# A hybrid S5 / neighbourhood-attention step on one core: a new order for its first stage

## The chip, the cores and the metric

The kernel runs on one core of one Trainium2 chip. The metric is the device time of one execution in microseconds (us). Five engines matter: PE (TensorE, matrix products, with PEld for its weight loads), DVE (VectorE), ACT (ScalarE), POOL (GpSimd) and SP (SyncE, which here only starts transfers). Each engine works through its own list of instructions in order; an instruction that waits for another engine or for a transfer holds up all that stands behind it in its list.

## The reference

One layer of a diffusion backbone for 384 tokens (256 of a sample, 128 of a prompt). What the change touches is the front of it: the modulation of the input by a condition, the root-mean-square norm, the first columns of the input projection, and the discretisation of the state-space tables.

```python
def _rms(x, w):
    y = xf * lax.rsqrt(jnp.mean(xf * xf, axis=-1, keepdims=True) + EPS)
    return (y * w.astype(jnp.float32)).astype(x.dtype)

def _modulation(cond, w_ada, b_ada):
    mod = jax.nn.silu(cond) @ w_ada + b_ada
    shift, scale, gate = jnp.split(mod[:, None, :], 3, axis=-1)

def _front(x, shift, scale, norm_w, w_in, q_norm_w, k_norm_w):
    h = _rms(x, norm_w) * (1 + scale) + shift
    proj = h @ w_in            # cut into u, z_s, q, k, v, z_a, g_s, g_a
    ...

def _s5_discretize(a_re, a_im, log_dt, b_re, b_im):
    lam = lax.complex(jnp.minimum(a_re.astype(f32), -1e-4), a_im.astype(f32))
    dt = jnp.exp(log_dt.astype(f32))[..., None]
    lam_bar = jnp.exp(lam * dt)
    b_bar = ((lam_bar - 1) / lam)[..., None] * b
    ...
```

Behind it come the state-space scan over u, the attention over q, k, v, gates from z_s, z_a, g_s and g_a, and the output projections. D_MODEL is 2048, the projection is 2048 x 10240, w_ada is 2048 x 6144, all in float32.

## The kernel before

**Precision.** Every float32 product of a weight w and an input h is made as three products of parts: `hi` (w rounded, by ACT) and `lo` (what is left, by a subtraction), and `hh`, `hl` of the input in the same way. So a step of the projection is hh·hi + hl·hi + hh·lo, lines 813, 814 and 815, each with a moving side of 384 tokens.

**First stage.** It makes u, z_s and half of g_s (3072 columns of `w_in`) while the modulation is still being computed. The contraction of 2048 is cut into nine slices: two of 128 rows (slices 0 and 1), then seven of 256 (slices 2 to 8). A slice's work is a list of units of 512 KB of `w_in` (2 units in slice 0, 4 in slice 1, 6 in each later one), each unit two half-units, each half-unit 12 products on PE. After them the result in PSUM (tile `m`, three buffers) goes to `ua`, `zs` or `gs`: copied in slices 0 and 1 where it is the first, added by DVE afterwards (line 147, `ua<-m,ua`). A slice's `hh` and `hl` need the modulation of that slice: products of the condition `ct` with `w_ada` (`ada_mm`, line 693, two or four groups a slice, one loaded tile `wa` each), a copy (`ada_sum`), a transpose (`ada_turn`, line 707), three small DVE operations (`ada_fin`), the modulation on ACT (`modulate`, tile `hf`), and the split into `hh` and `hl` (`split_h`, lines 731 and 147, both on DVE). The table `AHEAD` says in which half-unit n of a slice each of these steps for the next slice stands; `fn == "mm"` and `"turn"` come after the half-unit's products, the others before.

**Weights.** `Stream` loads `w_in` units into `raw` (four buffers), and `prep` makes `hi` on ACT and `lo` for each half-unit three half-units ahead; in this stage `lo` is made on POOL (`low_on_pool`), 128x512 each. All loads stand on SP's list: at the start x (tile `X`, three of 1 MB), five small vectors into `vn`, then `wa` and `raw` tiles. POOL's list begins with eleven small loads (the norm weights, and `a2`, `ld` for the tables). A transfer from SP, or ACT, takes one of eight semaphores in turn and waits until the earlier transfer on it has landed.

**Start.** ACT squares and sums each third of X (line 756), POOL takes the root, DVE scales X, PE turns all 16 column tiles of X (`turn_x`, line 775), copied back by ACT and DVE in turn. In this list stand the first two `ada_mm`, and behind all 16 tiles the first product of slice 0.

**Tables.** `ssm_setup` is a generator of some hundred DVE operations on 128x64 tiles (`expo`, sine and cosine, `cmul`). `Background` runs it: after every half-unit from slice 2 on `bg.step(0.6)` lets the generator go to its next `yield`, so that two to eight operations follow each other on DVE.

**End of the stage.** In slice 8 the finished `zs` and `gs` are gated: ACT takes the tanh of `zs` into a tile `sg` (a ring of six, shared), DVE makes the product into it, SP stores it (`zss`), two half-units after one another; `gs` likewise without the DVE step (`gss`). In the same half-units the state-space stage starts: `ssm_read` puts its loads on SP (C, then B in rows of 64 bytes into `x4b`, then U), between the `raw` units of the next block.

Behind the first stage come blocks of the projection and the output products, with the state-space scan and the attention beside them; the change leaves them as they are.

## Time and profile before

| what | value |
|---|---|
| time, median of 3 runs | 1227.48 us (1226.68 to 1229.29) |
| profiled execution, its own time | 1229.62 us |
| its span | 1227.8 us |
| PE busy | 1165.2 us (95%), 7215 products |
| DVE / ACT / POOL busy | 817.4 / 565.7 / 158.6 us |
| first product of slice 0 | 31.48 us into the span |
| end of the first stage | about 300 us |
| transfers | 217.38 MB, mean 177 GB/s |

The page lists each engine's busy time, the chain of work that ended last, the costliest groups of instructions and the transfers; the views behind it show single instructions in order of time with the idle time before each and what ended it. The profiled time lies 2.1 us above the median of the runs; differences are made against the profiled execution.

### The profile page before, as it was taken

The page shows a single profiled execution, that of the slowest core. Times are in us where ns is not written, and L with a number is a line of the kernel's source. Part 1 is how long each engine was busy: PE and PEld are TensorE (multiplying, and loading weights), DVE is VectorE, ACT ScalarE, POOL GpSimd, SP SyncE. Part 2 cuts the span into 40 slices and gives each one's busy share as a digit, 9 for nine tenths or more (in the row PEclk, how much of TensorE's full clock was granted, in tenths as well). Part 3 has the DMA queues.
Part 4 walks back from the last instruction along what each step waited for, and adds up shares of the span by engine and source line. Part 5 has one row for each costly group of instructions (what it writes and reads, how often), then busy time and mean ns, then how long its engine had stood idle before and what let it go on. Part 6 is the DMA issues. An engine that isn't in the chain of part 4 may idle for free.

```text
span 1227.8 us, 19705 instructions
## 1 busy us (share of the span) xinstructions
PE 1165.2 (95%) x7215; PEld 1016.4 (83%) x7215; DVE 817.4 (67%) x1957; ACT 565.7 (46%) x1027; POOL 158.6 (13%) x126
## 2 busy tenths in 40 slices
PE   3999999998999999999999999999898999999997
PEld 2787788897889888889999778877697899878886
DVE  3588775555649993454999344468778855687873
ACT  4432223334683339677334944455545433343332
POOL 2444444453000000000000001100100000000000
PEclk9999999998999999999999999999999999999999
DMA  9975557639428458424645353435654247896672
GB/s 265 347 258 202 203 197 236 228 119 242 156 69 199 134 156 161 130 82 113 169 149 161 97 164 115 146 102 167 208 153 146 93 159 255 259 296 215 216 235 81
DMA packets 216852, 217.38 MB, mean 177 GB/s; under 512 B 63977, under 2 KB 172129, under 8 KB 216372
## 3 DMA queue, kind: packets, MB, share of 16 engines
q1 hardware_dynamic: 216404, 215.93, 57.6%
q8 instruction: 57, 0.93, 0.3%
q0 software_dynamic: 352, 0.20, 0.2%
q14 instruction: 39, 0.32, 0.1%
HBM read 197.90 MB, written 16.87 MB: 175 GB/s over the span
## 4 chain that ended last, share of the span: by engine, by line
PE 75%; ACT 9%; DVE 9%; issue 3%; DMA 2%; SPq 0%; POOL 0%; DVEq 0%; ACTq 0%; POOLq 0%
PE m L192 10%; PE m L194 9%; PE m L193 9%; PE m L203 8%; PE m L205 7%; PE m L204 7%; PE m L813 5%; PE m L814 5%; PE m L815 5%; PE bk L693 3%; ACT H L456 2%; DVE lo L71 2%; ACT hi L70 1%; PE bk L445 1%; DMA X<-in_x_sample_dram 1%
## 5 line engine op out<-in xcount | busy, mean ns | idle before, releaser
L70 ACT ACTIVATE hi<-raw 128x512 fp32r<-128x512 f32 x464 | 286.9, 629 | 361.9 <-PE m L193 115.8
L71 DVE TENSOR_TENSOR lo<-raw,hi 128x512 fp32r<-128x512 f32 x367 | 250.2, 687 | 217.8 <-ACT hi L70 213.4
L192 PE MATMUL m<-hh,hi 128*128 128x384 f32 x832 | 288.0, 346 | 10.8 <-DVE ms L155 2.9
L194 PE MATMUL m<-hh,lo 128*128 128x384 f32 x832 | 280.6, 337 | 0.2
L193 PE MATMUL m<-hl,hi 128*128 128x384 f32 x832 | 279.7, 336 | 0.0
L203 PE MATMUL m<-hi,hh 128*128 128x512 f32 x480 | 190.0, 396 | 0.0
L205 PE MATMUL m<-hi,hl 128*128 128x512 f32 x480 | 187.3, 390 | 0.0
L204 PE MATMUL m<-lo,hh 128*128 128x512 f32 x480 | 187.1, 390 | 0.1
L192 PEld LDWEIGHTS m<-hh,hi 128*128 128x128 f32 x832 | 157.3, 189 | 24.7 <-ACT hi L70 5.4
L194 PEld LDWEIGHTS m<-hh,lo 128*128 128x128 f32 x832 | 157.3, 189 | 0.9 <-DVE lo L71 0.9
L193 PEld LDWEIGHTS m<-hl,hi 128*128 128x128 f32 x832 | 157.5, 189 | 0.1
L813 PE MATMUL m<-hh,hi 128*128 128x384 f32 x384 | 135.5, 353 | 16.5 <-DVE hh L731 7.5
L71 POOL TENSOR_TENSOR lo<-raw,hi 128x512 fp32r<-128x512 f32 x97 | 126.6, 1314 | 154.0 <-ACT hi L70 148.3
L814 PE MATMUL m<-hl,hi 128*128 128x384 f32 x384 | 131.0, 341 | 0.8 <-DVE hl L147 0.5
L815 PE MATMUL m<-hh,lo 128*128 128x384 f32 x384 | 130.9, 341 | 0.4 <-POOL lo L71 0.4
L203 PEld LDWEIGHTS m<-hi,hh 128*128 128x128 f32 x480 | 90.1, 188 | 21.8 <-issue 1.4
L205 PEld LDWEIGHTS m<-hi,hl 128*128 128x128 f32 x480 | 90.1, 188 | 19.0
L204 PEld LDWEIGHTS m<-lo,hh 128*128 128x128 f32 x480 | 90.2, 188 | 18.5 <-DVE lo L71 0.5
L813 PEld LDWEIGHTS m<-hh,hi 128*128 128x128 f32 x384 | 73.2, 191 | 32.1 <-ACT hi L70 8.8
L814 PEld LDWEIGHTS m<-hl,hi 128*128 128x128 f32 x384 | 73.7, 192 | 2.2 <-DVE hl L147 2.2
L815 PEld LDWEIGHTS m<-hh,lo 128*128 128x128 f32 x384 | 73.5, 191 | 0.9 <-POOL lo L71 0.9
L147 POOL TENSOR_TENSOR rm<-rn,mhalf 128x24 f32<-128x24 f32 x4 | 18.0, 4511 | 364.8 <-DVE rn L152 364.8
(264 smaller groups left out, 1288.3 us busy)
## 6 DMA issues: line engine op xcount, KB each, us to landing
raw<-in_w_in_dram SPq DMA_DIRECT2D x160, 512.0 KB, 4.1
wa<-in_w_ada_dram SPq DMA_DIRECT2D x32, 1024.0 KB, 5.5
gw<-in_w_ada_dram SPq DMA_DIRECT2D x32, 512.0 KB, 5.5
raw<-in_w_o_dram SPq DMA_DIRECT2D x32, 512.0 KB, 6.1
raw<-in_w_ssm_out_dram SPq DMA_DIRECT2D x16, 512.0 KB, 3.4
raw<-in_w_att_out_dram SPq DMA_DIRECT2D x16, 512.0 KB, 5.7
raw<-in_w_glu_dram SPq DMA_DIRECT2D x8, 512.0 KB, 4.5
tgs<-sg SPq DMA_DIRECT2D x16, 192.0 KB, 1.9
```

The lines of the kernel that those rows point to most:

```text
L70: self.nc.scalar.activation(h, t, AF.Copy)
L71: (self.nc.gpsimd if self.low_on_pool else self.nc.vector).tensor_tensor(l, t, f(h), op=OP.subtract)
L192: PE.matmul(o, wh[:, kk, w], xh[q][:, j, :], start=first and hb == 0 and kk == 0, stop=False)
L193: PE.matmul(o, wh[:, kk, w], xl[q][:, j, :], start=False, stop=False)
L194: PE.matmul(o, wl[:, kk, w], xh[q][:, j, :], start=False, stop=last and hb == 1 and kk == 1)
L203: PE.matmul(ps[r], xh[q][:, j, tk], wh, start=first and hb == 0, stop=False)
L204: PE.matmul(ps[r], xh[q][:, j, tk], wl, start=False, stop=False)
L205: PE.matmul(ps[r], xl[q][:, j, tk], wh, start=False, stop=last and hb == 1)
L693: PE.matmul(pab[b][32 * (k % 4):32 * (k % 4) + 32, 0:128 * nk], ct[:, kt, :], wa[s, i][:, k, :], start=kt < 4, stop=kt >= 12)
L813: PE.matmul(o, wh[:, w], hh[q][:, j, :], start=kk == 0, stop=False)
L814: PE.matmul(o, wh[:, w], hl[q][:, j, :], start=False, stop=False)
L815: PE.matmul(o, wl[:, w], hh[q][:, j, :], start=False, stop=kk == nk - 1)
```

## The change

It reorders the first stage and moves some of its work to other engines; the arithmetic stays.

- **Loads.** The five `vn` vectors are loaded from ACT's list, ahead of everything; both `wa` tiles of slice 0 stand before the first `raw`. `ssm_load` (six small loads) moves from POOL to ACT, after the second sum of squares; POOL's other five small loads stand behind the three roots.
- **Start.** The condition's part (`vt`, `ct`) is made after the first sum of squares. Of X only tiles 0 and 1 are turned before the first modulation, 2 to 5 before slice 0, and 6 to 15 one by one in slices 1 and 2 (new entry "x" in `AHEAD`). Fourteen steps of the table generator run before slice 0.
- **Condition's products.** From slice 2 on the four groups stand in two pairs (half-units 1 and 4) and the steps behind them end in half-unit 9, not 11.
- **Splits.** `split_h` makes `hh` on ACT and `hl` on POOL, except for tile 0.
- **Tables.** A `yield` follows every operation, so that one stands behind each half-unit, from slice 1 on; `cmul` handles two or three complex products in one operation (78 yields are left for the 80 half-units of slices 1 to 7).
- **Gates.** `zs` is gated in place, and `zss` and `gss` are stored from POOL's list, one half-unit later.

```diff
 def expo(pl, o, x, n):
         ts(r, x, -87.0, OP.max, 88.0, OP.min)
+        yield 0.6
         ts(k, r, 1.4426950408889634, OP.mult, MAGIC, OP.add)
+        yield 0.6
         ts(k, k, -MAGIC, OP.add)
         yield 0.6
...
     def cmul(pl, o, x, y):
...
-        tt(o[:, 0], x[:, 0], y[:, 0], OP.mult)
-        tt(t1, x[:, 1], y[:, 1], OP.mult)
-        tt(o[:, 1], x[:, 0], y[:, 1], OP.mult)
-        tt(t2, x[:, 1], y[:, 0], OP.mult)
-        tt(o[:, 0], o[:, 0], t1, OP.subtract)
-        tt(o[:, 1], o[:, 1], t2, OP.add)
+        tt(o, re, y, OP.mult)
+        yield 0.6
+        tt(t, im, y[:, :, ::-1], OP.mult)
+        yield 0.6
+        tt(o[:, :, 0], o[:, :, 0], t[:, :, 0], OP.subtract)
+        yield 0.6
+        tt(o[:, :, 1], o[:, :, 1], t[:, :, 1], OP.add)
+        yield 0.6
...
     def ssm_load(t):
-            GP.dma_start(a2[:, i], dram(a[n], 0, [[64, 64], [4096, 2], [1, 64]]))
+            S.dma_start(a2[:, i], dram(a[n], 0, [[64, 64], [4096, 2], [1, 64]]))
...
     def split_h(kt):
-        V.tensor_copy(hh[q][:, j, :], h2)
-        tt(hl[q][:, j, :], h2, f(hh[q][:, j, :]), OP.subtract)
+        if kt == 0:
+            V.tensor_copy(hh[q][:, j, :], h2)
+        else:
+            S.activation(hh[q][:, j, :], h2, AF.Copy)
+        tt(hl[q][:, j, :], h2, f(hh[q][:, j, :]), OP.subtract, eng=GP if kt else V)
...
+    vn = p1.tile([88, 128], F32, name="vn")
+    for n, r0, r1 in (("c", 0, 16), ("c_ctx", 16, 32), ("norm_w", 32, 48), ("b_ada", 48, 80), ("b_glu", 80, 88)):
+        S.dma_start(vn[r0:r1, :], dram(a[n], 0, [[128, r1 - r0], [1, 128]]))
     for r, (n, t0) in enumerate((("x_sample", 0), ("x_prompt", 0), ("x_sample", 128))):
         SP.dma_start(X[:, r], dram(a[n], t0 * D, [[D, 128], [1, D]]))
+    V.memset(ct, 0.0)
     load_ada(0, 0)
+    load_ada(0, 1)
     st.upto(1, 0)
-    load_ada(0, 1)
+    load_ada(1, 0)
+    st.upto(2, 0)
+    load_ada(1, 1)
+    st.upto(3, 0)
...
+    for r in range(3):
+        if r:
+            S.activation(junk, X[:, r], AF.Square, accum_out=ss[:, r:r + 1])
+        if r == 1:
+            s_in = ssm_load(p1)
+        ts(ss[:, r:r + 1], ss[:, r:r + 1], 1.0 / D, OP.mult, EPS, OP.add)
+        rsqrt_(rs[:, r:r + 1], ss[:, r:r + 1])
+        ts(X[:, r], X[:, r], rs[:, r:r + 1], OP.mult)
+    for t_, n_ in ((kwc, "k_norm_w"), (qwc, "q_norm_w")):
+        for h_ in range(2):
+            GP.dma_start(t_[64 * h_:64 * h_ + 64], dram(a[n_], 0, [[1, 64], [1, 1]]))
+    GP.dma_start(kw, dram(a["k_norm_w"], 0, [[0, 128], [1, 64]]))
...
-    turn_x(range(6))
     ada_mm(0, 0)
     ada_sum(0, 0)
-    turn_x(range(6, 8))
-    st.upto(3, 1)
+    turn_x(range(2))
     ada_mm(0, 1)
     ada_sum(0, 1)
-    for i in range(2):
-        load_ada(2, i)
     ada_turn(0)
     ada_fin(0)
     modulate(0)
     split_h(0)
-    turn_x(range(8, 16))
+    st.upto(3, 2)
+    for i in range(2):
+        load_ada(2, i)
+    set_ = ssm_setup(sp, *s_in, [p1.tile([128, TOK], F32, name=f"room{i}") for i in range(2)])
+    next(set_)
+    turn_x(range(2, 6))
+    for _ in range(13):
+        next(set_)
...
     def gate_zs(k):
-        stt(t, t, 1.0, zacc[k], OP.add, OP.mult)
-        yield -1
-        SP.dma_start(zss[k], t)
+        stt(zacc[k], t, 1.0, zacc[k], OP.add, OP.mult)
+        yield -2
+        GP.dma_start(zss[k], zacc[k])
...
     def gate_gs(k):
-        SP.dma_start(gss[k], gacc[k])
+        yield -2
+        GP.dma_start(gss[k], gacc[k])
...
-             {1: [("mm", 0)], 2: [("mm", 1)], 3: [("sum", 0), ("mm", 2)], 4: [("mm", 3)], 5: [("sum", 1), ("turn", 0)],
-              6: [("fin", 0), ("mod", 0)], 7: [("split", 0), ("mod", 1), ("split", 1)]}]
-    AHEAD += [{0: [("mm", 0)], 2: [("mm", 1)], 3: [("sum", 0)], 4: [("mm", 2)], 6: [("mm", 3)], 7: [("sum", 1)],
-               8: [("turn", 0)], 9: [("fin", 0), ("mod", 0)], 10: [("split", 0), ("mod", 1)], 11: [("split", 1)]}] * 6 + [{}]
+             {0: [("x", 6), ("mm", 0)], 1: [("x", 7), ("mm", 1)], 2: [("x", 8), ("sum", 0), ("mm", 2)],
+              3: [("x", 9), ("mm", 3)], 4: [("x", 10), ("sum", 1), ("turn", 0)], 5: [("x", 11), ("fin", 0), ("mod", 0)],
+              6: [("split", 0), ("mod", 1)], 7: [("split", 1)]}]
+    AHEAD += [{1: [("mm", 0), ("mm", 1)], 2: [("sum", 0)], 4: [("mm", 2), ("mm", 3)], 5: [("sum", 1), ("turn", 0)],
+               7: [("fin", 0), ("mod", 0)], 8: [("split", 0), ("mod", 1)], 9: [("split", 1)]} for _ in range(6)] + [{}]
+    for n in range(4):
+        AHEAD[2].setdefault(6 + n, []).append(("x", 12 + n))
...
-            bg.step(0.6 if s > 1 else 0)
+            bg.step(0.6 if s else 0)
```

PE's list from its start to the first products of slice 0, before (`vn` is turned first; `sg` holds the condition's products):

```order
L761 MATMUL bk<-ident,vn 128x88
L775 MATMUL bk<-ident,X 128x128 x18
L693 MATMUL bk<-wa,ct 32x128 x16
L775 MATMUL bk<-ident,X 128x128 x6
L693 MATMUL bk<-wa,ct 32x128 x16
L707 MATMUL bk<-ident,sg 128x128 x2
L775 MATMUL bk<-ident,X 128x128 x24
L813 MATMUL m<-hh_98,hi 128x384
```

and after (`a` is the tables' input `a2`; lines 818, 726, 740 and 854 are 775, 693, 707 and 813 of before):

```order
L792 MATMUL bk<-ident,vn 128x88
L726 MATMUL bk<-wa,ct 32x128 x16
L818 MATMUL bk<-ident,X 128x128 x6
L726 MATMUL bk<-wa,ct 32x128 x16
L740 MATMUL bk<-ident,sg 128x128 x2
L264 MATMUL bk<-ident,a_200 128x64 x4
L818 MATMUL bk<-ident,X 128x128 x12
L854 MATMUL m<-hh_98,hi 128x384
```

Thirty of the 48 turns of X left this part of the list, and both groups of the condition's products moved ahead of most of the others.

DVE's list at the border from slice 3 to slice 4, before (`gs` and `ua` are the additions from PSUM, `pw` and `cm` table operations):

```order
L147 TENSOR_TENSOR gs_134<-m,gs_134 128x384
L147 TENSOR_TENSOR gs_135<-m,gs_135 128x384
L147 TENSOR_TENSOR pw<-pw 128x64
L147 TENSOR_TENSOR cm_1476<-pw 128x64
L147 TENSOR_TENSOR pw<-pw 128x64
L147 TENSOR_TENSOR cm_1477<-pw 128x64
L147 TENSOR_TENSOR pw<-pw,cm_1476 128x64
L147 TENSOR_TENSOR pw<-pw,cm_1477 128x64
L731 CAST hh_99<-hf 128x384
L147 TENSOR_TENSOR hl_103<-hf,hh_99 128x384
L147 TENSOR_TENSOR gs_136<-m,gs_136 128x384
L147 TENSOR_TENSOR gs_137<-m,gs_137 128x384
```

and DVE's list at a slice's border after:

```order
L147 TENSOR_TENSOR gs_134<-m,gs_134 128x384
L147 TENSOR_TENSOR gs_135<-m,gs_135 128x384
L147 TENSOR_TENSOR room_293<-room_293,room_294 128x64
L147 TENSOR_TENSOR gs_136<-m,gs_136 128x384
L147 TENSOR_TENSOR gs_137<-m,gs_137 128x384
L327 RECIPROCAL room_293<-room_293 128x64
L147 TENSOR_TENSOR ua<-m,ua 128x384 x2
```

One table operation stands behind each pair of additions, and the split is gone from DVE.

POOL's list in the last two slices after (before, only `lo` stands here):

```order
L147 TENSOR_TENSOR hl_105<-hf,hh_101 128x384
L71 TENSOR_TENSOR lo<-raw,hi 128x512
L147 TENSOR_TENSOR hl_105<-hf,hh_101 128x384
L71 TENSOR_TENSOR lo<-raw,hi 128x512 x11
L866 DMA zss<-zs_123 128x384
L866 DMA zss<-zs_122 128x384
L71 TENSOR_TENSOR lo<-raw,hi 128x512
L866 DMA zss<-zs_125 128x384
L866 DMA zss<-zs_124 128x384
L71 TENSOR_TENSOR lo<-raw,hi 128x512
```

`hl` and the stores of `zs` now stand between the weight splits.

## Rows read from the trace of the kernel before

**Rows 1.** The page: busy time, share of the span and instructions of each engine

```profile
PE 1165.2 (95%) x7215; PEld 1016.4 (83%) x7215; DVE 817.4 (67%) x1957; ACT 565.7 (46%) x1027; POOL 158.6 (13%) x126
```

**Rows 2.** PE's waits from 0 to 300 us: for whom, total, times, longest

```profile
PE m L813 <- DVE hh L731: 7.5, 4, 2.5
```

**Rows 3.** PE in order of time: first product of slices 0, 1, 2, 3

```profile
31.48 0.42 PE L813 MATMUL m<-hh,hi 128*128 128x384 f32 x1
...
44.31 0.44 PE L813 MATMUL m<-hh,hi 128*128 128x384 f32 x1 [1.73 <-ACT zs L876]
...
68.89 0.44 PE L813 MATMUL m<-hh,hi 128*128 128x384 f32 x1 [0.76 <-DVE hh L731]
...
102.58 0.44 PE L813 MATMUL m<-hh,hi 128*128 128x384 f32 x1 [2.35 <-DVE hh L731]
```

**Rows 4.** PE: first product of slices 7 and 8, and what follows slice 8

```profile
234.78 0.44 PE L813 MATMUL m<-hh,hi 128*128 128x384 f32 x1 [0.69 <-DVE gs L147]
...
266.00 0.44 PE L813 MATMUL m<-hh,hi 128*128 128x384 f32 x1 [0.69 <-DVE gs L147]
...
300.13 0.63 PE L375 MATMUL bk<-ident,x4a 128*128 128x128 f32 x2
```

**Rows 5.** ACT: the sums of squares of the first and last third of X

```profile
5.75 1.91 ACT L756 ACTIVATE ua<-X 128x2048 f32<-128x2048 f32 x1 [3.73 <-DMA X<-in_x_sample_dram]
...
15.98 1.91 ACT L756 ACTIVATE ua<-X 128x2048 f32<-128x2048 f32 x1 [3.78 <-DMA X<-in_x_sample_dram]
```

**Rows 6.** Stretches at the start: length, busy (count) by engine, PEclk, DMA share, GB/s

```profile
3.00:6.00 3.00, 0.00 (x0) 0.00 (x0) 0.00 (x0) 0.25 (x1) 2.94 (x6) 1.00 0.94 382
6.00:12.00 6.00, 0.00 (x0) 0.00 (x0) 0.88 (x2) 3.56 (x3) 2.25 (x4) 1.00 0.79 195
...
21.00:27.00 6.00, 6.00 (x72) 5.03 (x74) 2.14 (x6) 2.16 (x6) 0.00 (x0) 1.00 1.21 291
```

**Rows 7.** POOL: the first of its small loads, and a later one

```profile
1.36 1.22 POOL L741 DMA_DIRECT2D kwc<-in_k_norm_w_dram  x2 [0.28 <-issue]
...
8.27 0.59 POOL L244 DMA_DIRECT2D a<-in_state_ssm_im_dram  x1 [2.33 <-DMA kwc<-in_k_norm_w_dram]
```

**Rows 8.** PE: six turns of X, and the second group of the condition's products

```profile
25.65 0.92 PE L775 MATMUL bk<-ident,X 128*128 128x128 f32 x6
26.50 1.08 PE L693 MATMUL bk<-wa,ct 128*32 128x128 f32 x32
```

**Rows 9.** The page's group of the weight splits on POOL: count, busy us, mean ns

```profile
L71 POOL TENSOR_TENSOR lo<-raw,hi 128x512 fp32r<-128x512 f32 x97 | 126.6, 1314 | 154.0 <-ACT hi L70 148.3
```

**Rows 10.** PE in slice 6: products, a group of the condition's products, the next product

```profile
206.29 0.33 PE L813 MATMUL m<-hh,hi 128*128 128x384 f32 x1
...
206.64 0.34 PE L815 MATMUL m<-hh,lo 128*128 128x384 f32 x1
206.91 1.07 PE L693 MATMUL bk<-wa,ct 128*32 128x256 f32 x16
207.91 0.44 PE L813 MATMUL m<-hh,hi 128*128 128x384 f32 x1
```

**Rows 11.** DVE at the border of slices 3 and 4: table operations

```profile
133.07 1.36 DVE L147 TENSOR_TENSOR pw<-pw 128x64 f32<-128x64 f32 x1
...
136.82 0.21 DVE L147 TENSOR_TENSOR cm<-pw 128x64 f32<-128x64 f32 x1
```

**Rows 12.** POOL in the same time

```profile
131.49 5.33 POOL L71 TENSOR_TENSOR lo<-raw,hi 128x512 fp32r<-128x512 f32 x4 [3.68 <-ACT hi L70]
```

**Rows 13.** DVE from 33 to 300 us by shape: count, busy us, mean ns, idle before

```profile
L147 DVE TENSOR_TENSOR gs<-m,gs 128x384 f32<-128x384 f32 x55 | 29.1, 552 | 10.4 <-PE m L815 10.4
```

**Rows 14.** ACT in slice 8: the wait for a buffer of `sg`

```profile
293.71 1.12 ACT L821 ACTIVATE sg<-zs 128x384 f32<-128x384 f32 x2 [9.72 <-DMA zss<-sg]
```

**Rows 15.** SP in slice 8: loads of B, and the next `raw` unit

```profile
280.43 4.60 SPq L343 DMA_DIRECT2D x4b<-in_ssm_b_re_dram  x2
...
288.14 1.07 SPq L51 DMA_DIRECT2D raw<-in_w_in_dram  x1
```

More of the change, by code (lines that the diff above doesn't have):

```diff
@@ L251, in ssm_setup @@
         lre, dt, mg, th, k, z = (room[0][:, 64 * i:64 * i + 64] for i in range(6))
-        iv, nu = (room[1][:, 128 * i:128 * i + 128].rearrange("p (r g) -> p r g", r=2) for i in range(2))
+        iv, nu = (room[1][:, 128 * i:128 * i + 128].rearrange("p (o r g) -> p o r g", o=1, r=2) for i in range(2))
         s_, c_ = (room[1][:, 256 + 64 * i:320 + 64 * i] for i in range(2))
@@ L298, in ssm_setup @@
+            yield from cmul(t, pw[:, 1:2], pw[:, 0:1], pw[:, 0:1])
+            yield from cmul(t, pw[:, 2:4], pw[:, 1:2], pw[:, 0:2])
             fw = t.tile([128, 4, 2, 64], F32, name="fw")
             tt(z, lre, lre, OP.mult)
+            yield 0.6
             tt(s_, aim, aim, OP.mult)
+            yield 0.6
             tt(z, z, s_, OP.add)
+            yield 0.6
             V.reciprocal(z, z)
-            tt(iv[:, 0], lre, z, OP.mult)
-            stt(iv[:, 1], aim, -1.0, z, OP.mult, OP.mult)
@@ L305, in ssm_setup @@
-            ts(nu[:, 0], pw[:, 0, 0], -1.0, OP.add)
-            V.tensor_copy(nu[:, 1], pw[:, 0, 1])
-            yield 1.4
-            cmul(t, fw[:, 0], nu, iv)
-            yield 1.2
-            for k_ in range(3):
-                cmul(t, fw[:, k_ + 1], fw[:, 0], pw[:, k_])
-                yield 1.2
-            for s in range(4):
-                V.tensor_copy(sp["me"][0:64, s], fw[0:64, 3 - s])
-                V.tensor_copy(sp["mc"][64:128, s], pw[64:128, 3 - s])
-                yield 0.3
+            yield 0.6
@@ new lines, in ssm_setup @@
+            tt(iv[:, 0, 0], lre, z, OP.mult)
+            yield 0.6
+            stt(iv[:, 0, 1], aim, -1.0, z, OP.mult, OP.mult)
+            yield 0.6
+            ts(nu[:, 0, 0], pw[:, 0, 0], -1.0, OP.add)
+            yield 0.6
+            V.tensor_copy(nu[:, 0, 1], pw[:, 0, 1])
+            yield 0.6
+            yield from cmul(t, fw[:, 0:1], nu, iv)
+            yield from cmul(t, fw[:, 1:4], fw[:, 0:1], pw[:, 0:3])
+            V.tensor_copy(sp["me"][0:64], fw[0:64, ::-1])
+            yield 0.6
@@ L325, in ssm_setup @@
             i8 = ident.rearrange("p (e b i) -> p e b i", b=2, i=16)
             V.tensor_reduce(sp["ev"][:, 0:1], i8[:, :, 0, :], axis=AX.XY, op=OP.add)
+            yield 0.6
             V.tensor_reduce(sp["ev"][:, 1:2], i8[:, :, 1, :], axis=AX.XY, op=OP.add)
[L328 removed]
+            yield 0.6
     prefetched = {}
@@ L798, in hybrid @@
     split_h(0)
-    turn_x(range(8, 16))
-    ts(qwc, qwc, 0.125, OP.mult)
+    st.upto(3, 2)
[6 more added lines that the diff above has]
+        next(set_)
     hb_ = const.tile([128, 8], F32, name="hbg")
     ts(hb_, vt[:, 80:88], 0.5, OP.mult)
-    g_set = bg.add(ssm_setup(sp, *s_in, [p1.tile([128, TOK], F32, name=f"room{i}") for i in range(2)]))
+    g_set = bg.add(set_)
     def mode_k(i, hb, nk, k0):
@@ L890, in hybrid @@
                     ada_turn(s + 1)
+                elif fn == "x":
+                    turn_x([j])
             i += hb
```

78 lines of the change are left out of this document (42 added, 36 removed).

## The prediction, made before the changed kernel ran

> **What bounds the kernel now.** I read the page's busy times first [rows 1]: PE is busy 95% of the span, so a change pays by the time in which PE stands still or does work that it could be spared. Then PE alone, from 0 to 300 us, for that is the stretch that the change touches. It has three parts. PE makes no product of the projection before 31.48 us [rows 3]. Then each slice has a pitch, from first product to first product: slice 1 24.58 us (44.31 to 68.89), slice 2 33.69 [rows 3], and slice 7, the same list as slice 2 but without the table operations beside it, 31.22 [rows 4]; slices 3 to 7 together take 163.42 us (102.58 to 266.00) [rows 3, 4]. Last, slice 8 takes 34.13 us (266.00 to 300.13) [rows 4] though it has no modulation to prepare. The products follow each other every 0.174 us (206.29 to 206.64 is two steps) [rows 10], so slice 8's 144 should take 25.0: 9.1 us are lost there. At the borders PE waits 7.5 us for `hh` on DVE [rows 2], 2.35 us of it before slice 3 [rows 3], and 0.69 us even where no table operation runs [rows 4].
>
> **The start.** The last third of X is there at 15.98 us, the first at 5.75 [rows 5]. Two thirds should need 2 x 1.05 MB at 382 GB/s, 5.5 us; they took 10.2, because from 6 to 12 us the transfers moved only 195 GB/s [rows 6], and in that time POOL's small loads, issued from 1.36 us on, were under way (the first landed after 8 us) [rows 7]. In the changed kernel none of them stands ahead of X, so I put X at 11.2. The two `wa` tiles follow at once, each 1.05 MB at 291 GB/s [rows 6], 3.6 us: 14.8 and 18.4. ACT is late for the last third: it issues six loads first, at about 0.6 us each by the price of two in 1.22 [rows 7], so square, root, scale and the two turns end near 18.7. The second group of the condition's products then starts at about 18.8 instead of 26.50 [rows 8], and by the 5.0 us from there to the first product (26.50 to 31.48) [rows 3, 8] slice 0 could begin at 23 to 24.
>
> It cannot run on. ACT's list has the `hi` of the second `raw` unit ahead of the copies out of PSUM, and with three buffers PE stops at its fourth result. Behind the `wa` tiles the first `raw` comes at 20.2, then `wa`, `raw`, `wa`, `raw` at 23.8, 25.6, 29.2 and 31.0 by the same 291 GB/s. POOL's five loads, now behind the third root, fall into that time. Before, 6 us at 195 instead of 382 GB/s cost 2.9 us [rows 6]; the bounds of the same traffic here are 0 and 2.9, I take 1.5, since half of the eleven loads went to ACT. So the second `raw` is there at 27.1, its `hi` and a copy (1.2 us, by the 1.12 of two ACT operations of 128x384 [rows 14]) free PE at 28.3. From there: a last result 0.5, a group of 1.1 [rows 8], a half-unit of 2.08 (12 products), a group, which makes 33.1, the third half-unit (its `raw` at 32.5 is in time within the three buffers), turn 0.5, the fourth, and the wait for the split as before (1.73 [rows 3], and 0.4 more as `hl` is on POOL): slice 1 begins at 39.9, before at 44.31. I take 4.4 us of gain; with nothing lost to the small loads it is 6, with loads never late 8.5, with the full 2.9 and a stall more 2.
>
> **Slices 1 and 2.** The ten tiles of X that left the start are now PE's work: three turns each, 0.15 us apiece [rows 8], 0.45, in slice 1 mostly beside another group. Slice 1 gets six, 2.2 us with shared refills, and loses the border wait of some 1.7 (0.76 [rows 3], the stalls around it and the split on DVE). Its half-units with four results load DVE with 4 x 0.55 = 2.2 us [rows 13] against 2.08 of products, and a table operation now comes on top: I take a loss of 1 us there in all, from 0 to 3. Slice 2 gets four tiles, 1.8 us.
>
> **Slices 2 to 7: the border wait.** Where it comes from is seen at the border of slices 3 and 4. Three table operations there take 1.36 us and less, where the fourth, of the same size, takes 0.21 [rows 11]; the long ones lie in a stretch in which POOL makes four `lo` without a pause [rows 12]. So DVE's operation waits for POOL's to end, and behind six of them in a row stand the split and the additions for which PE waits. The change takes all of that apart: the split leaves DVE, its steps end two half-units (over 4 us) before the border, and one table operation stands behind each pair of additions. POOL gets two `hl` a slice, 128x384, at 1.31 x 384/512 = 0.99 us each [rows 9], and is then busy 12 x 1.31 + 2 x 0.99 = 17.7 of some 29 us: it has room. I count the wait as gone.
>
> The price per slice starts from slice 7's 31.22. Off goes the border, 0.69 us idle [rows 4] and 0.2 of refill. Off goes one change of kind for each pair of groups: 206.64 to 206.91 is 0.27 where a product's step is 0.17, the product behind takes 0.44 and not 0.33 [rows 10]; that is 0.2 at least, and at most the 0.5 that the group's 1.27 us hold beyond its streaming; I take 0.4, twice a slice. So 31.22 - 0.9 - 0.8 = 29.5. Slices 3 to 7: 163.4 - 5 x 29.5 = **15.9** us of gain. Slice 2: 33.7 - 29.5 - 1.8 = **2.4**. What else a long wait costs PE afterwards is in the pitches, and goes with it.
>
> **The lock's new place.** A table operation of up to 1.36 us [rows 11] and two additions of 0.52 to 0.55 [rows 13] make 2.4 us, over the 2.08 of a half-unit; a short one makes 1.3. With three buffers PE bears about 1 us of delay, so single long ones cost nothing and only long ones in series do. In before most are short. I take 1.5 us for all 78, from 0 to 12 (a mean operation of 1.2 us: 78 x 0.15).
>
> The Trainium skill, "SBUF — State Buffer", section "SBUF: two separate sides", says that DVE (with two SBUF inputs, or in a two-port mode) and GpSimd share one port pair as an exclusive lock, held for the whole instruction, and the loser waits. The long rows at 133 us agree, and the additions from PSUM (0.55 us throughout) too. By this rule the change, which gives POOL more to do, could pay the lock at every operation; that is the second rival.
>
> **Slice 8.** ACT waits 9.72 us for a buffer of `sg` whose store has not landed [rows 14]; DVE's next product and the additions stand behind that, and `hi` for what follows. Gated in place, the ring is not held, and the stores are off SP's list. What is late next: the `raw` units of the next block. SP's issue of B's 64-byte rows takes from 280.43 to 288.1, and the next `raw` follows only then [rows 15]; PE needs it at about 295 in a slice without stops, and it would land in time by some tenths; the two behind it come up by the sixteen stores that left SP. POOL has two stores of about 0.6 us [rows 7] and one `lo` of 1.31 [rows 9] a half-unit, 2.5 us against 2.08, for three half-units, within its lead of three. I take 1.5 us of loss left, 0 to 9: a gain of **7.6**.
>
> **The sum.** 4.4 - 1.0 + 2.4 + 15.9 + 7.6 - 1.5 = 27.8 us. What follows the first stage is PE-bound and its list is the same, so it moves up as a whole. The profiled execution's 1229.6 becomes 1201.8; the median of the runs lies 2.1 below, so 1199.7: **1200 us**.
>
> **Rivals.** First, slice 8 stays late for another reason: B's rows and the stores share the transfer engines, and the `raw` units come no earlier. For it: SP's 7.6 us at B [rows 15]. Against it: PE's stop there had its end when a store landed, not a `raw`. Then 7.6 shrinks to about 0 to 1: **1207 us**. Second, the lock, and it is the one that ends on the other side: each table operation falls behind a `lo`, since after two additions a half-unit's `lo` has just begun. DVE then needs 1.04 us plus the operation per half-unit, and PE follows DVE wherever the operation is over 1.04. At 1.2 us it costs 12 us: 1210. Gain and loss are even at a mean of 1.04 + (27.8 + 1.5)/78 = 1.42 us; at 1.5, as the merged `cmul` of two to six times the size might be with the wait, it costs 36 instead of 1.5: **1234 us**, slower than before. Against it: the long rows reach only 1.36, and the fourth row beside them is 0.21 [rows 11]. Third, the start gives nothing: the slow transfers from 6 to 12 us have another cause, or ACT's issues take longer: **1204 us**. Fourth, the borders move instead of vanishing (DVE's additions late for another reason, `hl` late behind `lo`), and slices 2 to 7 give half of their 18.3: **1209 us**.
>
> **How the numbers follow.** The forecast (1191 to 1205) has 0.63, the first rival 0.12, the third 0.07, the fourth 0.07, the lock at 1.2 us 0.05; the lock above its point 0.03, and 0.03 that several of these cancel the gain (1225 to 1230). A measurement of this kernel can tell about 0.2%, 2.5 us. Faster by more: 0.94; within: 0.03; slower: 0.03. The range takes in the forecast's better ends (the start 8.5, no lock, slice 8 without loss: 1191) and reaches to the rivals at 1204 to 1210: 1191 to 1210.
>
> **What would show it.** The first sum of squares of the last third of X near 13 to 14 us; the first product of slice 0 at 23 to 24 with a stop behind it; slice 1 from about 40; pitches of 31.3 in slice 2 and 29.5 in 3 to 7 with no wait for `hh`; slice 8 in 26 to 27 us; no wait of ACT on `zss`; the stage over at some 272 us. Long table operations one behind each pair of additions, and PE waiting for `ua`, `zs` or `gs` on DVE, would show the second rival; ACT's `hi` waiting for `raw` in slice 8 the first. A stage after 300 us that takes longer than before would make the prediction wrong in a way that I have no term for.

## The result, and the profile after

The changed kernel takes 1209.26 us (median of four runs, 1207.75 to 1211.18), the kernel before 1227.2: ratio 0.9842, 95% interval 0.9824 to 0.9859. The forecast was 1200 with a range of 1191 to 1210, so the time lies in the range, at its slow end: of the 27.8 us that the sum gave, 18 came. The profiled execution took 1211.18 us (span 1209.4), 1.9 above the median.

The page's line of busy times, to be held against [rows 1]:

```profile
PE 1159.6 (96%) x7215; PEld 1019.6 (84%) x7215; DVE 784.9 (65%) x1896; ACT 571.3 (47%) x1042; POOL 176.8 (15%) x150
```

TensorE alone, in order of time: the first product of the projection, then the same five products of its list that [rows 3, 4] show of before, then what follows slice 8.

```profile
25.02 0.67 PE L854 MATMUL m<-hh,hi 128*128 128x384 f32 x1
...
40.20 0.44 PE L854 MATMUL m<-hh,hi 128*128 128x384 f32 x1 [0.80 <-DVE zs L918]
...
68.37 0.33 PE L854 MATMUL m<-hh,hi 128*128 128x384 f32 x1
...
99.28 0.33 PE L854 MATMUL m<-hh,hi 128*128 128x384 f32 x1
...
216.03 0.33 PE L854 MATMUL m<-hh,hi 128*128 128x384 f32 x1
...
245.61 0.33 PE L854 MATMUL m<-hh,hi 128*128 128x384 f32 x1
...
272.43 0.60 PE L408 MATMUL bk<-ident,x4a 128*128 128x128 f32 x4
```

One correction of the prediction's marks belongs here. I had called the product at which a border stop ends the first of a slice. Counted through the list (48, 96, then seven times 144 products), the row at 44.31 is the third before the end of slice 0, those at 68.89 and 102.58 are the fourth of slices 2 and 3, and those at 234.78 and 266.00 the sixth before an end. The table compares the same products in both kernels, so its gains hold. The forecast beside them does not quite fit the marks: 15.9 sets five whole slices of 29.5 against a stretch of before that is nine products (1.6 us) short of five slices, and 7.6 reckons slice 8 with 144 products where its stretch has 150 (1.0 us). These two nearly cancel. Counted in whole slices, slice 1 lost 4.2 us, and the gains are 1.7 in slice 2, 19.7 in slices 3 to 7 (167.6 to 147.9) and 7.2 in slice 8.

| stretch of TensorE's list | before | after | gain | forecast |
|---|---|---|---|---|
| to the end of slice 0 | 44.31 | 40.20 | 4.1 | 4.4 |
| slice 1 | 24.58 | 28.17 | -3.6 | -1.0 (0 to -3) |
| slice 2 | 33.69 | 30.91 | 2.8 | 2.4 |
| slices 3 to 7 | 163.42 | 146.33 | 17.1 | 15.9, less 1.5 for the lock |
| slice 8 | 34.13 | 26.82 | 7.3 | 7.6 |
| **first stage** | 300.13 | 272.43 | **27.7** | 27.8 |
| **what follows, to the end of the span** | 927.7 | 937.0 | **-9.3** | 0 |

The first stage did what the sum said, to a tenth of a microsecond in total, but with errors that cancel (slice 1 lost 2.6 us more than said, the lock cost less), so that the tenth is luck. The stage behind it, of which I had said that it moves up as a whole, became 9.3 us longer. TensorE's waits from 0 to 280 us (for whom, total, times, longest) show that the wait for `hh` [rows 2] is gone; by the first product of each slice, counted, slices 3 to 7 take 29.57 to 29.58 us each, forecast 29.5:

```profile
PE m L854 <- ACT ua L920: 1.4, 1, 1.4
PE m L854 <- DVE ua L918: 1.4, 1, 1.4
PE m L854 <- DVE zs L918: 0.8, 1, 0.8
PE m L854 <- ACT zs L920: 0.7, 1, 0.7
...
PE m L855 <- POOL hl L147: 0.3, 1, 0.3
```

All of these fall between 25 and 43 us. So two questions were left: which parts of the change the gain in the stage hangs on, and where the 9.3 us behind it went.

### The profile page after: what moved, and what is told of

Same layout as the page of the kernel before. It is cut to its first block, busy times and chain, and to the rows that moved or that the text cites. A ratio compares the mean times of both kernels' runs of the same rounds, so it can differ in the third digit from the quotient of the medians.

```text
span 1209.4 us, 19648 instructions
## 1 busy us (share of the span) xinstructions
PE 1159.6 (96%) x7215; PEld 1019.6 (84%) x7215; DVE 784.9 (65%) x1896; ACT 571.3 (47%) x1042; POOL 176.8 (15%) x150
## 4 chain that ended last, share of the span: by engine, by line
PE 78%; ACT 8%; DVE 7%; DMA 3%; issue 3%; SPq 1%; POOL 0%; DVEq 0%; ACTq 0%; POOLq 0%
PE m L192 10%; PE m L194 9%; PE m L193 9%; PE m L203 8%; PE m L205 8%; PE m L204 8%; PE m L854 5%; PE m L856 5%; PE m L855 5%; PE bk L726 2%; DVE lo L71 2%; ACT H L489 1%; PE bk L478 1%; ACT hi L70 1%; PE bk L1025 1%
## 5 line engine op out<-in xcount | busy, mean ns | idle before, releaser
L192 PE MATMUL m<-hh,hi 128*128 128x384 f32 x832 | 288.7, 347 | 13.5 <-ACT hi L70 5.0
L854 PEld LDWEIGHTS m<-hh,hi 128*128 128x128 f32 x384 | 72.6, 189 | 13.5 <-issue 6.2
```

Of the source, the lines that this page charges most:

```text
L192: PE.matmul(o, wh[:, kk, w], xh[q][:, j, :], start=first and hb == 0 and kk == 0, stop=False)
L854: PE.matmul(o, wh[:, w], hh[q][:, j, :], start=kk == 0, stop=False)
```

## The experiments

Times are medians; the ratio to the kernel before, run beside each, is given with its interval, since the runs of before differ by some 4 us between the groups (medians 1226.9 to 1231.3). "Stage" is the time at which the first stage ends in the profile.

### The borders: bursts, split, and the port between VectorE and GpSimd

**u_table**: the changed kernel with the table generator of before (the fourteen steps that are done ahead of slice 1 stay there).

```
         ts(r, x, -87.0, OP.max, 88.0, OP.min)
-        yield 0.6
         ts(k, r, 1.4426950408889634, OP.mult, MAGIC, OP.add)
-        yield 0.6
         ts(k, k, -MAGIC, OP.add)
         yield 0.6
...
-        tt(o, re, y, OP.mult)
-        yield 0.6
-        tt(t, im, y[:, :, ::-1], OP.mult)
-        yield 0.6
...
+        tt(o[:, 0], x[:, 0], y[:, 0], OP.mult)
+        tt(t1, x[:, 1], y[:, 1], OP.mult)
+        tt(o[:, 1], x[:, 0], y[:, 1], OP.mult)
+        tt(t2, x[:, 1], y[:, 0], OP.mult)
...
-    for _ in range(13):
+    for _ in range(4):
         next(set_)
```

> The changed kernel with the table generator of before (three to six operations behind one step, the small cmul), all else as changed. Theory (the bursts were the cause of the border stops, since whatever stands behind them on VectorE comes late, the split or the additions): slices 3 to 7 get longer than the 29.58 us that they take in the changed kernel, by 1 to 3 us each as long as tables run, 5 to 12 us in all. Rival (only the split, which stood behind the bursts, was the victim, and it now lies on other engines): pitches stay at 29.6, 0 to 1 us in all. The stage after 300 us of before: no difference expected by either.

Measured: 1227.3 us, ratio 0.9991 (0.9976 to 1.0007): the whole gain is gone. Stage 291.0. Slices 0 to 3 take 18.2, 28.0, 36.6 and 38.5 us (after: 16.7, 26.2, 30.9, 29.6), and from slice 4 on, where the tables are done, 29.6 to 29.9. The bursts were the cause, and cost more than the 5 to 12 us that I expected. The split, which is on ScalarE and GpSimd here, is no victim any more; the copies and additions behind the bursts are (TensorE waits 8.7 us for `gs`, 5.9 for `ua`). The edit takes back the merged `cmul` too, 32 operations more on VectorE; spreading and merging were not tried apart.

**u_split**: the changed kernel with the split on VectorE.

```
-        if kt == 0:
+        if True:
             V.tensor_copy(hh[q][:, j, :], h2)
...
-        tt(hl[q][:, j, :], h2, f(hh[q][:, j, :]), OP.subtract, eng=GP if kt else V)
+        tt(hl[q][:, j, :], h2, f(hh[q][:, j, :]), OP.subtract, eng=V)
```

> The changed kernel with both steps of the split on VectorE again (as before), table operations still one at a time. Theory (bursts): 4 x 0.4 to 0.6 us more on VectorE per slice find room, the step is issued two half-units ahead, pitches of slices 3 to 7 stay within 0.3 us of 29.58; 0 to 1.5 us in all. Rival (the split's engine was what mattered): a wait for hh on VectorE of 0.7 us or more returns at each border, 4 to 10 us in all.

Measured: 1222.1 us, ratio 0.9943 (0.9928 to 0.9958), 13 us slower than the changed kernel; stage 284.5, slices 3 to 7 at 33.5, 29.8, 32.0, 33.8 and 30.7. My theory said 1.5 at most, and fell; the rival was right in the size, though the wait was not for `hh` but for `gs` (6.5 us in five stops): the additions stand behind the split. Why it costs so much is in VectorE's rows of this run, the split at 124 us and the one at 23 us (start, duration in us):

```profile
22.76 0.36 DVE L765 CAST hh<-hf 128x384 fp32r<-128x384 f32 x1 [1.12 <-ACT hf L759]
23.16 0.56 DVE L147 TENSOR_TENSOR hl<-hf,hh 128x384 fp32r<-128x384 f32 x1
...
124.01 1.46 DVE L765 CAST hh<-hf 128x384 fp32r<-128x384 f32 x1
125.51 1.50 DVE L147 TENSOR_TENSOR hl<-hf,hh 128x384 fp32r<-128x384 f32 x1
126.94 1.01 DVE L147 TENSOR_TENSOR gs<-m,gs 128x384 f32<-128x384 f32 x2
```

and GpSimd in the second stretch:

```profile
121.04 5.56 POOL L71 TENSOR_TENSOR lo<-raw,hi 128x512 fp32r<-128x512 f32 x4 [3.44 <-ACT hi L70]
```

The same two operations take 0.92 us where GpSimd rests and 2.96 where it makes `lo`. The additions, with one operand in PSUM, take 0.5 each beside `lo` as elsewhere. The Trainium skill, "SBUF — State Buffer", section "SBUF: two separate sides", describes this as an exclusive lock on a port pair that GpSimd shares with VectorE's two-port operations and those with two SBUF inputs, held for a whole instruction; these rows agree.

**t_lodve**: u_table with `lo` on VectorE, so that GpSimd has next to nothing to do in the stage.

```
-    st.low_on_pool = True
```

> The changed kernel with the table generator of before (as u_table, 1227 us) and the low halves of the weights, lo, made on VectorE in the first stage and not on GpSimd: 8.3 us more work for VectorE per slice of 144 products, and none of GpSimd's. Theory (VectorE's operations wait for GpSimd's lo to end, and that is what makes the bursts long): table operations take 0.2 us again, slices 2 and 3 fall from 36.6 and 38.5 to 33 or less, and the whole gets 8 us or more faster than u_table. Rival (the bursts delay by their number and the wait for GpSimd is small): VectorE is only fuller, slices 2 and 3 stay or get longer, 0 to 16 us slower.

Measured: 1211.5 us, ratio 0.9857 (0.9841 to 0.9872). VectorE has twelve operations of 0.7 us more per slice and the old bursts, and the kernel is 15.8 us faster than u_table. Slices 2 and 3 take 31.0 and 31.7 us instead of 36.6 and 38.5. The same piece of the table in the two runs, first u_table (VectorE, then GpSimd beside it), then t_lodve:

```profile
102.28 1.34 DVE L147 TENSOR_TENSOR pw<-pw 128x64 f32<-128x64 f32 x1
103.54 1.32 DVE L147 TENSOR_TENSOR cm<-pw 128x64 f32<-128x64 f32 x1
104.79 1.30 DVE L147 TENSOR_TENSOR pw<-pw 128x64 f32<-128x64 f32 x1
106.01 0.21 DVE L147 TENSOR_TENSOR cm<-pw 128x64 f32<-128x64 f32 x1
...
102.24 3.77 POOL L71 TENSOR_TENSOR lo<-raw,hi 128x512 fp32r<-128x512 f32 x3
```

```profile
94.57 0.22 DVE L147 TENSOR_TENSOR pw<-pw 128x64 f32<-128x64 f32 x1
94.70 0.22 DVE L147 TENSOR_TENSOR cm<-pw 128x64 f32<-128x64 f32 x1
...
94.97 0.22 DVE L147 TENSOR_TENSOR cm<-pw 128x64 f32<-128x64 f32 x1
```

Three operations behind three `lo` in turn, 1.3 us each; without `lo`, 0.22. This settles the cause: a burst is long because each of its operations can let one `lo` go first. What the number of its operations costs by itself is small: in slices 2 and 3 together t_lodve takes 2.2 us more than the changed kernel, u_table 14.6.

**b_two**: the kernel before with these two parts alone, the table one operation at a time and the split moved (the places of the split as changed, four single groups of the condition's products).

> The kernel before with two parts of the change alone: table operations one at a time (fourteen of them ahead of the second slice, as changed), and the split on ScalarE and GpSimd two half-units earlier. Loads at the start, turns of X, gates, and single groups of the condition's products stay as before. Theory (these two together take the border stops away and carry most of the change; u_table and u_split each showed that one without the other does not): slices 3 to 7 at 30.2 us as in u_pair, against 33.5 on average before, 16 us in all, slice 2 some 2 us, start and slice 8 as before: 1227.5 - 18 = 1210, from 1207 to 1214. Rival (the two help only beside the other parts, above all the start's order and the gates): less than 9 us of gain, over 1218.

Measured: 1218.9 us, ratio 0.9902 (0.9878 to 0.9926), a gain of 12 us and so between the two. Slices 2 to 7 fall from 200.2 to 183.2 us by count, 17 us of the 18 that the theory said, with 30.2 for slices 3 to 5. But slice 0 got 4.8 us longer (13.5 to 18.3), which I had not counted: thirteen table operations now stand there on VectorE, beside `lo`, ahead of the copies out of PSUM. A stop of 3.0 us and, behind it, half clock from 39.9 to 43.3 us (1.7 us) account for nearly all of it. TensorE's stop there, and one of the operations:

```profile
39.81 0.66 PE L852 MATMUL m<-hh,hi 128*128 128x384 f32 x1 [3.02 <-DVE ua L913]
```

```profile
33.48 1.26 DVE L152 TENSOR_SCALAR ek<-er 128x64 f32<-128x64 f32 x1
```

**u_pair**: the changed kernel with single groups of the condition's products in slices 2 to 7.

```
-    AHEAD += [{1: [("mm", 0), ("mm", 1)], 2: [("sum", 0)], 4: [("mm", 2), ("mm", 3)], 5: [("sum", 1), ("turn", 0)],
+    AHEAD += [{1: [("mm", 0)], 2: [("mm", 1)], 3: [("sum", 0)], 4: [("mm", 2)], 5: [("mm", 3)], 6: [("sum", 1), ("turn", 0)],
```

> The changed kernel with the four groups of the condition's products in slices 2 to 7 one per half-unit instead of two and two. The step of the prediction says 0.4 us (0.2 to 0.5) for each pair taken apart, two pairs in six slices: 4.8 us slower (2.4 to 6.0), slices 3 to 7 at 30.4 instead of 29.58. Rival (a change of kind costs nothing, the 0.27 us row is a matter of how ends are modelled): 0.

Measured: 1213.1 us, ratio 0.9874 (0.9855 to 0.9892). The intervals of this and of the changed kernel touch, so the verdict is the profile's: slices 2 to 7 take 4.3 us more in all, 0.36 for each of twelve pairs (slice 3 30.23, after 29.58). In TensorE's rows, first u_pair, a single group; then the changed kernel, a pair:

```profile
171.10 0.34 PE L856 MATMUL m<-hh,lo 128*128 128x384 f32 x1
171.37 1.07 PE L726 MATMUL bk<-wa,ct 128*32 128x256 f32 x16
172.37 0.44 PE L854 MATMUL m<-hh,hi 128*128 128x384 f32 x1
172.65 0.34 PE L855 MATMUL m<-hl,hi 128*128 128x384 f32 x1
```

```profile
170.23 0.34 PE L856 MATMUL m<-hh,lo 128*128 128x384 f32 x1
170.50 1.93 PE L726 MATMUL bk<-wa,ct 128*32 128x256 f32 x32
172.36 0.44 PE L854 MATMUL m<-hh,hi 128*128 128x384 f32 x1
172.64 0.33 PE L855 MATMUL m<-hl,hi 128*128 128x384 f32 x1
```

From the product ahead to the second behind: 1.55 us for one group, 2.41 for two. Less the two steps of 0.17 that the products take anyway, that is 1.20 and 2.06, and 2 x 1.20 - 2.06 = 0.34.

### Behind the stage: where 9.3 us went

**u_gate**: the changed kernel with the gates of before (ring of `sg`, stores on SyncE).

```
-        stt(zacc[k], t, 1.0, zacc[k], OP.add, OP.mult)
-        yield -2
-        GP.dma_start(zss[k], zacc[k])
+        stt(t, t, 1.0, zacc[k], OP.add, OP.mult)
+        yield -1
+        SP.dma_start(zss[k], t)
...
-        yield -2
-        GP.dma_start(gss[k], gacc[k])
+        yield -1
+        SP.dma_start(gss[k], gacc[k])
```

> The changed kernel with the gates of before (ring of sg, stores issued by SyncE, three steps and not four). Theory (slice 8's stop moved behind the stage as late raw units, and the gates' extra step shifted the order of the products of the next stage): slice 8 takes some 33 us again, 7 us more, but of that 4 us come back behind it (no late raw unit, no half clock) and some 3 us in the second half of the SSM: 0 to 3 us slower than the changed kernel. Rival (the two are unrelated): 7 us slower.

Measured: 1209.9 us, ratio 0.9851 (0.9834 to 0.9867), the same as the changed kernel. Slice 8 takes 32.2 us again (after 25.8, both by count), the stage ends at 278.8, and what follows takes 927.9 us, as before. So in the changed kernel the new gates were worth nothing in all: the 6.3 us won in the stage were lost behind it. The old wait, and its price on TensorE (waits of ScalarE and of TensorE from 246 to 279 us):

```profile
ACT sg L862 <- DMA zss<-sg: 9.2, 1, 9.2
```

```profile
PE m L854 <- ACT hi L70: 4.6, 1, 4.6
```

**s0**: the changed kernel with one number altered. A gate's last step (in `gate_zs`, shown, and in `gate_gs`) takes 0.1 from the credit of the background work; with one step more per gate than before this moved the steps of the state-space scan (SSM), and with them half-units of 12 products, in TensorE's list at four places between 274 and 690 us.

```
         GP.dma_start(zss[k], zacc[k])
-        yield 0.1
+        yield 0
```

> The changed kernel with one number altered: the last step of the sixteen gates costs the background work nothing instead of 0.1. TensorE's products then stand in the order of before again behind the first stage (in the changed kernel a half-unit of 12 products is one place away in four places between 274 and 690 us). Theory (the shifted order costs the 3.0 us that TensorE loses between 650 and 709 us, waits for x4a and a stretch at half clock): 3 us faster than the changed kernel, 0 to 4. Rival (those 3 us are the chance of where the clock falls): 0, with the waits for x4a still there. The late raw unit at 286 us stays by both.

Measured: 1204.5 us, ratio 0.9801 (0.9784 to 0.9817), clear of the changed kernel's interval, some 5 us faster, a little over the theory's 4. TensorE's waits in the second half of the SSM, from 636 to 712 us, in the changed kernel and in s0:

```profile
PE bk L597 <- ACT x4a L586: 2.9, 2, 1.6
```

```profile
PE bk L597 <- ACT x4a L586: 0.3, 1, 0.3
```

ScalarE is busy there without a pause in either, with states (`x4a`, `x4b`) and `hi`; a half-unit of products less at the end leaves TensorE with nothing to put in their place. With the stretch at half clock behind the wait (687.8 to 691.2 us, absent in s0) the changed kernel loses 3.0 us between 674 and 726 us of before, and s0 none. It is no accident of one profile: set against the same products of before, all five profiles with the shifted order (the changed kernel, u_table, u_split, t_lodve, u_pair) lose 3.0 to 3.7 us there, and the eight with the order of before at most 0.1. The other 2 of the 5 agree with the clock elsewhere (granted in the four runs of each: 0.989 to 0.993 in the changed kernel, 0.993 to 0.997 in s0), without being traced to a place. Against u_gate, which has the same order of products, the new gates are now worth 5.4 us.

**s0_ulate**: s0 with the loads of `U` and `Dm` three steps later in SyncE's list. TensorE's list is the same.

```
+        if hf == 0:
+            bg.add(ssm_read_u(hf, x, uv, 3), True)
+            for _ in range(4):
+                yield -1
+        else:
+            yield from ssm_read_u(hf, x, uv, 0)
+
+    def ssm_read_u(hf, x, uv, late):
+        g0 = 32 * hf
+        for _ in range(late):
+            yield -1
         for g2 in range(2):
             for s in range(4):
                 SP.dma_start(x["U"][64 * g2 + 16 * s:64 * g2 + 16 * s + 16],
```

> As the run before (gates' last step at no cost), and the eight loads of U and the two of D of the first half go three steps later into SyncE's list, behind three raw units; TensorE's list is the same. Theory (the raw unit is late because SyncE stands at the loads of U, whose turn in the queue comes only as others land): the wait of 2.30 us for hi and the half clock behind it (1.7 us) go, 4 us faster than s0 (2 to 4.5). Rival (the transfer engines are full from 272 to 287 us at 312 GB/s, whoever stands first): the raw unit lands as late, or U does and TensorE waits at its products instead; 0, or up to 3 us slower.

Measured: 1201.6 us, ratio 0.9780 (0.9763 to 0.9798); its runs (1200.9 to 1203.9) and those of s0 beside it (1203.4 to 1205.7) overlap by half a microsecond, and the medians are 2.8 apart. What follows the stage falls from 930.7 to 926.5 us in the profiles. SyncE's list, first the changed kernel, then s0_ulate (start, time from the first to the last issue, count):

```profile
272.11 7.60 SPq L381 DMA_DIRECT2D U<-us  x4
279.80 0.40 SPq L51 DMA_DIRECT2D raw<-in_w_in_dram  x1
```

```profile
266.78 3.27 SPq L51 DMA_DIRECT2D raw<-in_w_in_dram  x3
270.10 3.44 SPq L392 DMA_DIRECT2D U<-us  x4
...
278.50 6.84 SPq L392 DMA_DIRECT2D U<-us  x4
```

In the changed kernel the `raw` unit stands behind four loads of `U`, is issued at 279.80, and TensorE waits for its `hi`:

```profile
288.26 0.55 PE L192 MATMUL m<-hh,hi 128*128 128x384 f32 x1 [2.30 <-ACT hi L70]
...
289.47 0.52 PE L192 MATMUL m<-hh,hi 128*128 128x384 f32 x1
289.79 0.52 PE L193 MATMUL m<-hl,hi 128*128 128x384 f32 x1
```

2.30 us, and then products 0.32 apart, half clock, until 291.9. In s0 the raw unit is as late (issued at 281.21, the waits there 1.2 us for `hi` and 1.6 for `E`). Set against the same products of before, the changed kernel loses 4.2 us in this stretch, s0 4.1 and s0_ulate nothing. In s0_ulate none of these waits is there, and the loads of `U` still take 6.84 us to issue; nobody waits for them. The transfer engines are full in that time (272 to 287 us, DMA share and GB/s at the end of the row), and with them full the order on the queue decides who is late (changed kernel):

```profile
272.00:287.00 15.00, 13.96 (x84) 13.58 (x82) 6.20 (x12) 4.77 (x10) 6.39 (x12) 1.00 1.12 312
```

**s0_stlate**: s0 with the sixteen stores of the gates ten steps later (`yield -12` for `yield -2`).

> As s0, with the sixteen stores of the gates ten steps (some 21 us) later, out of the stretch from 264 to 287 us; SyncE's and TensorE's lists are the same. Theory of the full engines: 3.1 MB less in that stretch, 10 us at 312 GB/s, so the raw unit lands in time, the wait and the half clock go: 4 us faster than s0, unless the stores are in the way later. Theory of SyncE's order: its loads of U still stand ahead of the raw unit, but come through faster; 1 to 2 us of the 4.

Measured: 1203.5 us (1199.6 to 1203.9), ratio 0.9783 (0.9758 to 0.9807), 0.9 faster than s0, which the runs don't tell from nothing. It doesn't decide what it was meant for: GpSimd has no other work behind the stage that would hold the stores, so they moved by 10 us at the first and 5 at the last, not 21, and still fell into the stretch. Its profile leaves the stores a share: the wait of 1.2 us for `hi` is gone and the stretch loses 2.3 us, not 4.1, but the stage ends 1.5 us later, with a stretch at half clock from 33.8 us that s0 has not. How much of the late `raw` unit is due to the stores is open.

### The start, and two attempts at slice 0

**s0_small**: s0 with the eleven small loads on GpSimd ahead of everything again.

> The run s0 with the eleven small loads (norm weights, the SSM's states) on GpSimd ahead of everything again, as before; the order of the large loads stays. Theory (they slow the transfers of X from 6 to 12 us): X's last third lands at about 15.9 instead of 11.2 us, the first product comes near 28 instead of 25 us, slice 1 begins 3 us later, and the whole is 2 to 4 us slower than s0 (1204.5). Rival (the slow stretch had another cause, or slice 0 waits for the raw units anyway): X lands within 1 us of 11.2 or slice 1 begins within 1 us of 41.7; 0 to 1 us.

Measured: 1208.8 us, ratio 0.9856 (0.9828 to 0.9883), slower than s0 by 4 us by the medians, by 7 by the ratios. The stretch from 6 to 12 us, and ScalarE's square of the last third of X:

```profile
6.00:12.00 6.00, 0.38 (x1) 0.18 (x1) 0.00 (x0) 2.30 (x5) 1.64 (x3) 1.00 0.80 201
```

```profile
16.08 1.91 ACT L808 ACTIVATE ua<-X 128x2048 f32<-128x2048 f32 x1 [2.17 <-DMA X<-in_x_sample_dram]
```

201 GB/s (s0: 382) and 16.08 us, as in [rows 5, 6] of before, with nothing else changed: the small loads slow the large ones there. First product 27.8 (s0 24.9), slice 1 from 45.2 (41.7). At the stage's end 2.0 of the 3.6 us are left, since slice 1 gets 1.5 shorter: the stretch at half clock with which it begins in s0 (43.1 to 46.5) is absent.

**best_lodve** is s0_ulate with `lo` on VectorE in the first stage, **best_split1** is s0_ulate with the split of the second k-tile on VectorE.

> The run s0_ulate (1201.6) with lo made on VectorE in the first stage. By what t_lodve showed, nothing waits for GpSimd any more: the scale of the second slice (am) takes 0.15 and not 1.19 us, slice 0 gets 1 us shorter, the half clock at its end goes with it or not: 1 to 3 us faster. Rival (VectorE is then too full: two additions, a lo and a table operation are 2.0 us of the 2.08 of a half-unit): slices 3 to 7 go above 29.58 us, 1 to 8 us slower.

> The run s0_ulate (1201.6) with the split of the second k-tile on VectorE, as the first's is. Theory (slice 1 waits for the chain hf, hh on ScalarE, hl on GpSimd): hh 0.16 and hl 0.44 us shorter by the rows of either engine, TensorE's waits at the border of slices 0 and 1 fall by some 0.6 us, and if the half clock behind them goes too, by 2.3: 0.5 to 2.5 us faster. Rival (the waits there are for buffers in PSUM, which the other engines empty late): 0.

Measured: 1202.5 us (ratio 0.9804, 0.9778 to 0.9830) and 1200.4 (0.9792, 0.9762 to 0.9821); neither can be told from s0_ulate. In best_lodve slices 3 to 7 take 29.57 to 29.58 us again: with table operations one at a time VectorE has room for `lo`, and it doesn't matter who makes it. At the end of slice 0 the two waits for `zs` are 0.43 and 0.74 us, after 0.81 and 0.70 in s0_ulate: `am` behind `lo` accounts for 0.4 us of them at most. Slices 0 and 1 together take 43.6 us, after 43.8. In best_split1 slice 0 is 1.6 us longer and slice 1 2.1 shorter, with the half clock earlier (28.3 to 35.1). The fastest kernels, best_split1, s0_ulate, best_lodve and s0_stlate, lie from 1200 to 1204 us and are not told apart by the runs, against 1209.3 of the changed one.

## Why the prediction was right, and where it failed

The first stage came out for the reasons given. The whole did not: the measured 1209 lies 4 us outside the forecast's own bounds (1191 to 1205), and inside the range only because that was drawn out to 1210 for the rivals, none of which came true at the place it named. That a loss of 9.3 us without a term still fell inside is luck.

**The start: right.** X's last third is squared at 13.81 us (13 to 14 forecast), the second `raw` lands at 27.4 (27.1), and the gain is 4.1 (4.4). ScalarE's row:

```profile
13.81 1.91 ACT L803 ACTIVATE ua<-X 128x2048 f32<-128x2048 f32 x1 [2.00 <-issue]
```

The first product is a microsecond later than said (25.0 for 23 to 24). That the transfers of X were slow because of the small loads, which I had only inferred, is shown by s0_small.

**Slice 1: mis-sized**, -3.6 for -1.0. The missing 2.6 us stand behind the product at 40.20: TensorE stops for 0.70 us (`zs`) and 0.26 (`hl`), and then runs at half clock from 42.7 to 46.1 us, which costs 1.7 and for which the prediction has no term. The two waits of 1.4 us for `ua` lie ahead of that product and count in the row above. What makes the stops is not shown. The lock is at work in slice 0: VectorE runs table operations there behind GpSimd's `lo`, and later the scale of slice 1 (rows of VectorE in the changed kernel, then GpSimd):

```profile
28.26 3.58 DVE L155 SCALAR_TENSOR_TENSOR room<-room,er 128x64 f32<-128x64 f32 x6
...
38.29 1.19 DVE L147 TENSOR_TENSOR am<-m,vt 128x2 f32<-128x2 f32 x1
```

```profile
28.17 2.55 POOL L71 TENSOR_TENSOR lo<-raw,hi 128x512 fp32r<-128x512 f32 x2 [7.99 <-ACT hi L70]
...
38.18 1.28 POOL L71 TENSOR_TENSOR lo<-raw,hi 128x512 fp32r<-128x512 f32 x1 [2.03 <-ACT hi L70]
```

But best_lodve, in which GpSimd makes no `lo`, wins nothing there: slices 0 and 1 together take 43.6 us, in s0_ulate 43.8 (in best_split1 43.4).

**The border wait and the price per slice: right**, 29.58 us for 29.5. The cause was right too (VectorE's operations behind `lo`), and the runs add what the prediction didn't say: the two parts only work together. Without the single table operations all of the gain is gone, without the moved split two thirds of it. Part of the price was the clock: in before it falls to half for 3.4 us behind three of the borders (104.3, 138.4 and 172.6 us), 1.7 us each, and in the changed kernel nowhere in slices 2 to 8. **The lock's new place**: nothing in slices 3 to 7, which hold two to four table operations over 0.45 us each and take the same 29.57 to 29.58 us as in best_lodve, where GpSimd makes no `lo`. That my 1.5 us were paid in slice 0 instead is not shown. The second rival, 1.42 us a piece, was far off: 23 of the 91 table operations took over 0.45 us, the longest 1.33, and the 78 in slices 1 to 7 took 0.39 on average. **The pairs**: 0.36 us for 0.4.

**Slice 8: right in itself**, 7.3 for 7.6 (6.5 with the 150 products of its stretch). The first rival named the right mechanism, late `raw` units, and I had put it inside slice 8; it came 13 us after its end.

**What follows the stage: wrong.** The step that failed is the sentence that it "is PE-bound and its list is the same, so it moves up as a whole". The prediction had named a longer stage after 300 us as what would make it wrong without a term, and so it came. Its list is not the same: a step more per gate moved the SSM's work, 3 us, or 5 with what the runs show of the clock; the two lists would have shown that beforehand, had I compared them past the first stage. And it does not begin free: with slice 8 no longer stopping, the loads of `B`, `U`, the stores and the weights came upon one another behind it; 2.30 us of wait and 1.7 of half clock, and s0_ulate gives 2.8 us of it back by the medians, 4.2 in the profiles. The third piece, 2.7 us between 914 and 921 us, is the clock alone (below), and lies in this profile, not in every one. The three (3.0, 4.2 and 2.7) make 9.9 us; against them stands 1.0 us that before loses to half clock at the head of this stretch (to 302.2 us), and some 0.4 is not traced. With the first two mended (s0_ulate) the time is 1201.6 us, within 2 of what the sum said.

## What to carry to other kernels

VectorE's operations waited here for whole instructions of GpSimd, so that short ones in a burst were paid at the length of the other engine's. Where two engines can hold each other up like this, spread the short ones, one at a time, between operations that are not held up, or let one engine do both kinds of work. A stop that is taken away at the end of a stage comes back at the next thing in the queue: look at who stands in front of the critical loads there. And where a cost or a step count steers a planner, compare the order of the whole program, not of the stage that was edited.
